# S5 scan in a hybrid decoder layer: a fifth step for each unit, and ScalarE copies into block form

## Chip, core and metric

The kernel runs on one core of one Trainium2 chip. The metric is the device time of one execution in microseconds; the profile beside it is one execution with its own time. In the views PE is TensorE, PEld its weight loads, DVE is VectorE, ACT is ScalarE, POOL is GpSimd, and SP is the engine that issues the loads.

## What is computed

One decoder layer on 512 tokens of width 2048 in float32. The change touches only the S5 mixer, a diagonal state space with 64 groups of 16 channels and 64 complex states per group. From the reference, cut:

```
A_bar = exp(A * dt);  B_bar = ((A_bar - 1) / A)[..., None] * Bm
Bu = einsum('gpc,btgc->btgp', B_bar, u)
states_t = A_bar * states_(t-1) + Bu_t
y = real(einsum('gcp,btgp->btgc', Cm, states)) + d * u
out = gelu(y) * sigmoid(gelu(y) @ w_glu + b_glu)
```

Beside it stand an mLSTM mixer (four heads), the common output projection, and a gated convolution MLP with two products of width 5504, which take most of the time.

## The kernel before

**The products.** Every large product is done in three passes of float32 (`mm3`, L207): a weight chunk of 128 x 1024 is loaded by SP (`wdma`, L142), ScalarE casts it to the high part, and VectorE subtracts to get the low part (`split`, L112, its rows are L115 and L116). `wget` (L160) splits two chunks ahead of the one that is multiplied, and three chunk buffers take turns. A chunk is 24 matmuls of 128 x 512. The stages are, in order: `u` (the S5 inputs), `xm`, `v`, `o`, `glu`, `ws` and `wm` (output projection, S5 part and mLSTM part), then the MLP (`gv`, `down`, `last`).

**The woven work.** After a chunk the loop calls `pump` (L193), which lets each generator in `side` do one step; a generator ends a step with `yield`. The S5 generator is `s5` (L454). It enters the list first and runs alone until stage `v`, from where two generators are served at each pump: `s5` and then `gates` (L671, the mLSTM gate products), later the `head` generators (L805). Nothing but these calls sets the order of the work: each engine gets its instructions in the order in which the code emits them.

**A unit of S5.** The loop at L575 goes over eight units (u = 0 to 7) of four groups of state pairs each, plus a last round u = 8 that only reads out. A unit has four steps; I name them A to D.

- A (L577 to L583): `taps` of the unit before (L566: PE turns Kt, L569 adds D on VectorE, five ScalarE copies L571 fill Tm), `u_turn` (PE turns the unit's inputs, ScalarE copies U), and `first` (L522): six small products on VectorE and then W by `cmul_to` (L513).
- B (L585 to L596): `readout` of the unit before (L544: twelve matmuls `py`, which need Sr, Si, the products with C of the unit before, and Tm), eight transposes `pw` of Wr and Wi with two ScalarE copies `xb`, and `second` (L536): the products of A and C (CAr, CAi), again by `cmul_to`.
- C (L598 to L621): sixteen matmuls `px`, six VectorE operations L611 to L616 on them with the phases Er and Ei that POOL makes ahead (`phases`, L463), and `turn_back` (L557, `pyt`).
- D (L623 to L640): matmuls `pkt`, two scans L629 and L630, and six products L633 to L638 that make Sr and Si.

`cmul_to` is called twice a unit. For each of its two outputs it multiplies twice into the buffers `t4[0]` and `t4[1]` (L516, L517) and then writes the sum or difference straight into block form, in which the two groups of a pair lie side by side on their own 64 partitions:

```
for k in range(2):
    p0 = slice(64 * k, 64 * k + 64)
    V.tensor_tensor(out=v5(o)[p0, :, :, k, :], in0=t4[0][p0], in1=t4[1][p0], op=op)
```

These are two instructions of 64 x 256 for each output (L520).

Of the kernel before, what the change touches and what calls it, by code (L numbers as in the profile page):

```python
# [53 lines left out]
def trunk(ctx: ExitStack, tc: tile.TileContext, A: dict, out: bass.AP):  # L54
    nc = tc.nc
    V, S, G, PE = nc.vector, nc.scalar, nc.gpsimd, nc.tensor
# [15 lines left out]
    def pair(i, dt):  # L72
        return sl.tile([P, 2 * T], dt, tag=f"p{i}", name=f"p{i}")
# [7 lines left out]
    p0, p1, p2 = [pair(i, F32) for i in range(3)]  # L81
# [4 lines left out]
    def slot(dt=F32, name="s"):  # L86
        q = mosubs if name in ("MOh", "MOl") else () if name == "acc" else subs[dt]
        if q:
            t = q.popleft()
            owner[id(t)] = (q, t)  # L90
        else:
            i = free.popleft()
            cnt[0] += 1
            t = sl.tile([P, T], dt, tag=f"s{i}", name=f"{name}_{cnt[0]}")
            owner[id(t)] = (i, t)
        return t

    def drop(*ts):
        for t in ts:
            i = owner.pop(id(t))[0]  # L100
            if isinstance(i, int):
                free.append(i)
            else:
                i.append(t)
# [25 lines left out]
    def vcol(n, i=0, w=1):  # L130
        c = VCOL[n] + i
        return vec[:, c:c + w]
# [307 lines left out]
    def v5(t):  # L440
        return t.rearrange("p (r j g c) -> p r j g c", r=4, j=4, g=2)

    def v3(t, n=4):
        return t.rearrange("p (r n) -> p r n", r=n)
# [9 lines left out]
    def s5():  # L454
# [38 lines left out]
        def fetch(u):  # L493
            bcs.append(slot(name="bc"))
            nc.sync.dma_start(out=bcs[-1][:, 0:256], in_=A["s5bc"][u])

        def coeffs(u):

            pr = slice(4 * u, 4 * u + 4)
            bc, ct = bcs.popleft(), slot(name="ct")  # L500
            if u < 7:
                fetch(u + 1)
            b4 = bc[:, 0:256].rearrange("p (q r c) -> p q r c", q=4, r=4)
            bt = bc[:, 256:512].rearrange("p (q r c) -> p q r c", q=4, r=4)
            t4 = [ct[:, i * 256:(i + 1) * 256].rearrange("p (r j c) -> p r j c", r=4, j=4) for i in range(2)]

            def pb(ap):
                return ap[:, pr].unsqueeze(2).to_broadcast([P, 4, 16])

            def ap4(ri):  # L510
                return afw[:, ri, pr, :].unsqueeze(3).to_broadcast([P, 4, 4, 16])

            def cmul_to(o_r, o_i, ar, ai, br, bi):  # L513
                br, bi = [x.unsqueeze(2).to_broadcast([P, 4, 4, 16]) for x in (br, bi)]
                for o, (x1, y1), (z1, w1), op in ((o_r, (ar, br), (ai, bi), SUB), (o_i, (ar, bi), (ai, br), ADD)):
                    V.tensor_tensor(out=t4[0], in0=x1, in1=y1, op=MUL)  # L516
                    V.tensor_tensor(out=t4[1], in0=z1, in1=w1, op=MUL)  # L517
                    for k in range(2):
                        p0 = slice(64 * k, 64 * k + 64)
                        V.tensor_tensor(out=v5(o)[p0, :, :, k, :], in0=t4[0][p0], in1=t4[1][p0], op=op)  # L520

            def first():  # L522
                w0r, w0i = W0
                V.tensor_tensor(out=bt[:, 0], in0=pb(w0r), in1=b4[:, 0], op=MUL)
                V.tensor_tensor(out=bt[:, 1], in0=pb(w0r), in1=b4[:, 1], op=MUL)
                V.tensor_tensor(out=bt[:, 2], in0=pb(w0i), in1=b4[:, 1], op=MUL)
                V.tensor_tensor(out=bt[:, 3], in0=pb(w0i), in1=b4[:, 0], op=MUL)
                V.tensor_tensor(out=bt[:, 0], in0=bt[:, 0], in1=bt[:, 2], op=SUB)
                V.tensor_tensor(out=bt[:, 1], in0=bt[:, 1], in1=bt[:, 3], op=ADD)
                cmul_to(Wr, Wi, ap4(2), ap4(3), bt[:, 0], bt[:, 1])  # L530
                for k in range(2):
                    p0 = slice(64 * k, 64 * k + 64)
                    S.activation(out=cd[p0, 0, :, k, :], in_=b4[p0, 2], func=AF.Copy)
                    S.activation(out=cd[p0, 1, :, k, :], in_=b4[p0, 3], func=AF.Copy, scale=-1.0)

            def second():  # L536
                cmul_to(CAr, CAi, ap4(0), ap4(1), b4[:, 2], b4[:, 3])
                V.tensor_tensor(out=v3(Dt[96:128, :]), in0=eye96[96:128, :].unsqueeze(1).to_broadcast([32, 4, 32]),
                                in1=vcol("d96", 4 * u, 4)[96:128].unsqueeze(2).to_broadcast([32, 4, 32]), op=MUL)
                drop(bc, ct)  # L540

            return first, second
# [23 lines left out]
        def taps():  # L566
            pk = aux_ps("pk")
            PE.transpose(out=pk[:, 0:P], in_=Kt, identity=ident)
            V.tensor_tensor(out=tm[:, :, 3, :], in0=v3(pk[:, 0:P]), in1=v3(Dt), op=ADD)  # L569
            for jo, d0, s0, n in ((2, 0, 32, 32), (2, 32, 64, 32), (2, 64, 96, 32), (1, 0, 64, 64), (0, 0, 96, 32)):  # L570
                S.copy(out=tm[d0:d0 + n, :, jo, :], in_=tm[s0:s0 + n, :, 3, :])  # L571
# [3 lines left out]
        for u in range(9):  # L575

            if u > 0:  # L577
                taps()
            if u < 8:
                u_turn(u)  # L580
                first, second = coeffs(u)
                first()
            yield  # L583

            if u > 0:  # L585
                yt = readout(u - 1)
            if u < 8:
                XB = []
                for w in (Wr, Wi):
                    pw = aux_ps("pw")  # L590
                    for r in range(4):
                        PE.transpose(out=pw[:, r * P:(r + 1) * P], in_=w[:, r * P:(r + 1) * P], identity=ident)
                    XB.append(slot(name="xb"))
                    S.copy(out=XB[-1], in_=pw)
                second()
            yield  # L596

            if u < 8:  # L598
                px = []
                for xb in XB:  # L600
                    p_ = aux_ps("px")
                    for r in range(4):
                        w = slice(r * P, (r + 1) * P)
                        PE.matmul(p_[:, w], lhsT=xb[:, w], rhs=U[u][:, w], start=True, stop=True)
                    px.append(p_)
                drop(*XB)
                Er, Ei, Rd = nxt
                if u < 7:
                    nxt = phases(u + 1)
                ta, tb, vr, vi = slot(name="ta"), slot(name="tb"), slot(name="vr"), slot(name="vi")  # L610
                V.tensor_tensor(out=ta, in0=px[0], in1=Er, op=MUL)  # L611
                V.tensor_tensor(out=vi, in0=px[0], in1=Ei, op=MUL)
                V.tensor_tensor(out=tb, in0=px[1], in1=Ei, op=MUL)
                V.tensor_tensor(out=vr, in0=ta, in1=tb, op=ADD)
                V.tensor_tensor(out=tb, in0=px[1], in1=Er, op=MUL)
                V.tensor_tensor(out=vi, in0=vi, in1=tb, op=SUB)  # L616
            if u > 0:
                turn_back(u - 1, yt)
            if u == 8:
                break  # L620
            yield  # L621

            pkt = aux_ps("pkt")  # L623
            for q, w in ((0, Wr), (1, Wi)):
                for r in range(4):
                    PE.matmul(pkt[32 * r:32 * r + 32, 0:P], lhsT=cd[:, q, r].rearrange("p g c -> p (g c)"),
                              rhs=w[:, r * P:(r + 1) * P], start=(q == 0), stop=(q == 1))
            S.copy(out=Kt, in_=pkt[:, 0:P])
            V.tensor_tensor_scan(out=ta, data0=Rd, data1=vr, initial=0.0, op0=MUL, op1=ADD)  # L629
            V.tensor_tensor_scan(out=tb, data0=Rd, data1=vi, initial=0.0, op0=MUL, op1=ADD)  # L630
            e0 = slice(0, P - 1)
            e_r, e_i, s_r, s_i, ra, rb = [v3(x)[:, :, e0] for x in (Er, Ei, ta, tb, vr, vi)]
            V.tensor_tensor(out=ra, in0=e_r, in1=s_r, op=MUL)  # L633
            V.tensor_tensor(out=rb, in0=e_i, in1=s_i, op=MUL)
            V.tensor_tensor(out=v3(Sr)[:, :, 1:P], in0=ra, in1=rb, op=ADD)
            V.tensor_tensor(out=ra, in0=e_r, in1=s_i, op=MUL)
            V.tensor_tensor(out=rb, in0=e_i, in1=s_r, op=MUL)
            V.tensor_tensor(out=v3(Si)[:, :, 1:P], in0=ra, in1=rb, op=SUB)  # L638
            drop(ta, tb, vr, vi, Rd, Er, Ei)
            yield  # L640
# [387 lines left out]
    for c in range(8):  # L1028
        wh, wl = wget()
        for j in range(4):  # L1030
            for q in range(2):
                k = 2 * c + q
# [398 lines left out]
    for m in range(MD, 16):  # L1431
        pt = acc_ps("down")
        for c in range(KD // 8):
            d_dma(j + 2)
            while spill:
                o, a = spill.popleft()
# [197 lines left out]
```

## Time and profile before

| what | value |
|---|---|
| median of 3 runs | 2118.34 us (2117.73 to 2120.08) |
| the profiled execution, its own time | 2120.67 us |
| its span, first to last instruction | 2118.9 us |
| mean granted clock of TensorE | 0.987 |
| busy: PE / DVE / ACT / POOL | 2067.7 / 1507.2 / 799.2 / 290.0 us |

The span is cut by stage below with one row for a stretch: busy time of each engine in it, the granted clock, and the load on the DMA engines. What PE isn't busy in a stretch it waited. S5 runs from about 80 to 354 us.

### The profile page before, as it was taken

What the parts mean: (1) busy time and instruction counts of PE and PEld (TensorE: products, weight loads), DVE (VectorE), ACT (ScalarE), POOL (GpSimd) and SP (SyncE); (2) the same over time, 40 slices, a digit from 0 to 9 for tenths busy, and PEclk for the clock granted to TensorE, in tenths of its full rate; (3) what the DMA queues carried; (4) which work ended last, traced back from release to release, by engine and by line L of the source; (5) the groups of instructions that cost most, each with busy time, mean ns of one, the idle gap of its engine ahead of it and who ended that gap; (6) DMA issues with size and microseconds to landing.
All of it is one profiled execution on the core that took longest, in us unless ns stands there. A gap on an engine that the chain in (4) does not pass through costs nothing.

```text
span 2118.9 us, 31328 instructions
## 1 busy us (share of the span) xinstructions
PE 2067.7 (98%) x12956; PEld 1881.7 (89%) x12956; DVE 1507.2 (71%) x2017; ACT 799.2 (38%) x946; POOL 290.0 (14%) x511
## 2 busy tenths in 40 slices
PE   8999989999999999999999999999999999999997
PEld 7887778888888799999999999999998888888887
DVE  7699996458655788989889898898886544222235
ACT  5244433345424543333443334333343432111124
POOL 4877660001101200000000000000000000000003
PEclk9999999999999989999999999999999999999999
DMA  4222113222333323333433333333332555333352
GB/s 172 83 73 76 63 53 110 82 87 80 115 139 115 136 103 119 111 110 114 135 110 110 120 120 119 120 110 111 118 131 90 188 174 190 110 110 113 119 199 80
DMA packets 75369, 244.73 MB, mean 115 GB/s; under 512 B 8397, under 2 KB 14029, under 8 KB 64217
## 3 DMA queue, kind: packets, MB, share of 16 engines
q1 hardware_dynamic: 75224, 242.72, 33.5%
q8 instruction: 101, 1.65, 0.3%
q14 instruction: 44, 0.35, 0.0%
HBM read 220.12 MB, written 22.57 MB: 115 GB/s over the span
## 4 chain that ended last, share of the span: by engine, by line
PE 80%; DVE 13%; POOL 2%; issue 2%; ACT 2%; DMA 1%; SPq 0%; DVEq 0%; ACTq 0%; POOLq 0%
PE gv L210 14%; PE gv L208 14%; PE gv L209 13%; PE down L209 7%; PE down L210 7%; PE down L208 7%; DVE a L116 2%; PE o L208 1%; PE ws L208 1%; PE ws L210 1%; PE o L210 1%; PE o L209 1%; PE ws L209 1%; PE v L208 1%; PE v L210 1%
## 5 line engine op out<-in xcount | busy, mean ns | idle before, releaser
L210 PE MATMUL gv<-T,a 128*128 128x256 f32 x2408 | 687.2, 285 | 4.4 <-DVE a L1157 4.4
L208 PE MATMUL gv<-T,a 128*128 128x256 f32 x2408 | 683.7, 284 | 4.0 <-ACT a L1153 4.0
L209 PE MATMUL gv<-T,a 128*128 128x256 f32 x2408 | 683.0, 284 | 0.0
L210 PEld LDWEIGHTS gv<-T,a 128*128 128x128 f32 x2408 | 463.9, 193 | 9.6 <-DVE a L1157 4.9
L208 PEld LDWEIGHTS gv<-T,a 128*128 128x128 f32 x2408 | 464.1, 193 | 4.5 <-ACT a L1153 4.5
L1153 ACT CAST a<-a 128x3584 fp32r<-128x3584 f32 x86 | 274.8, 3196 | 502.9 <-DVE a L1149 373.1
L209 PEld LDWEIGHTS gv<-T,a 128*128 128x128 f32 x2408 | 464.1, 193 | 0.0
L116 DVE TENSOR_TENSOR a<-a,a 128x1024 fp32r<-128x1024 f32 (+2 forms) x205 | 238.6, 1166 | 302.1 <-ACT a L115 301.1
L1157 DVE TENSOR_TENSOR a<-a,a 128x3584 fp32r<-128x3584 f32 (+2 forms) x88 | 336.2, 3822 | 82.7 <-ACT a L1153 82.6
L115 ACT CAST a<-a 128x1024 fp32r<-128x1024 f32 (+2 forms) x205 | 198.7, 973 | 379.6 <-PE down L209 296.1
L1486 POOL TENSOR_TENSOR c<-c,c 128x256 f32<-128x256 f32 x24 | 17.8, 741 | 1339.3 <-ACT c L1484 1338.4
L208 PE MATMUL down<-c,a 128*128 128x512 f32 x448 | 175.4, 392 | 4.0 <-ACT c L115 4.0
L210 PE MATMUL down<-c,a 128*128 128x512 f32 x448 | 175.0, 391 | 0.0
L209 PE MATMUL down<-c,a 128*128 128x512 f32 x416 | 162.9, 392 | 0.1
L1147 DVE TENSOR_TENSOR a<-a 128x1024 f32<-128x1024 f32 x86 | 104.8, 1219 | 0.0
L208 PEld LDWEIGHTS down<-c,a 128*128 128x128 f32 x448 | 84.6, 189 | 22.1 <-ACT c L115 4.4
L210 PEld LDWEIGHTS down<-c,a 128*128 128x128 f32 x448 | 84.7, 189 | 17.6
L209 PEld LDWEIGHTS down<-c,a 128*128 128x128 f32 x416 | 78.6, 189 | 16.9 <-DVE c L116 0.7
L209 PE MATMUL down<-a,a 128*128 128x512 f32 x176 | 68.5, 389 | 0.0
L208 PE MATMUL down<-a,a 128*128 128x512 f32 x176 | 68.5, 389 | 0.0
L1218 DVE SCALAR_TENSOR_TENSOR p<-p,vec,p 128x511 f32<-128x511 f32 x86 | 62.5, 748 | 2.5 <-ACT p L1211 0.9
L1149 DVE TENSOR_TENSOR a<-a 128x512 f32<-128x512 f32 x86 | 60.5, 703 | 2.9
(589 smaller groups left out, 3608.1 us busy)
## 6 DMA issues: line engine op xcount, KB each, us to landing
a<-in_wgv SPq DMA_DIRECT2D x86, 1024.0 KB, 4.8
a<-in_wdB SPq DMA_DIRECT2D x55, 512.0 KB, 3.4
a<-in_wdA SPq DMA_DIRECT2D x40, 320.0 KB, 3.2
hidd<-p SPq DMA_DIRECT2D x40, 256.0 KB, 6.2
a<-in_wxm SPq DMA_DIRECT2D x16, 512.0 KB, 3.3
a<-in_wv SPq DMA_DIRECT2D x16, 512.0 KB, 3.2
a<-in_wo SPq DMA_DIRECT2D x16, 512.0 KB, 3.2
a<-in_wouts SPq DMA_DIRECT2D x16, 512.0 KB, 3.5
```

The costliest lines, as they stand in the source:

```text
L115: S.copy(out=h, in_=src)
L116: V.tensor_tensor(out=l, in0=src, in1=f(h), op=SUB)
L208: PE.matmul(pt, lhsT=wh, rhs=xh, start=first, stop=False)
L209: PE.matmul(pt, lhsT=wh, rhs=xl, start=False, stop=False)
L210: PE.matmul(pt, lhsT=wl, rhs=xh, start=False, stop=last)
L1147: V.tensor_tensor(out=v[:, 4:6], in0=v[:, 0:1].to_broadcast([P, 2, T]), in1=v[:, 1:3], op=ADD)
L1149: V.tensor_tensor(out=v[:, 0], in0=v[:, 6], in1=v[:, 3], op=ADD)
L1153: S.copy(out=part(RH[s % 2], lo, hi - lo), in_=part(RS[s % 2], lo, hi - lo))
L1157: V.tensor_tensor(out=part(RL[s % 2], lo, hi - lo), in0=part(RS[s % 2], lo, hi - lo), in1=f(part(RH[s % 2], lo, hi - lo)), op=SUB)
L1218: V.scalar_tensor_tensor(out=y1[:, s:], in0=gs[:, 0:T - s], scalar=vcol("f_cw", 3 * (k0 + j) + 2 - s), in1=y1[:, s:], op0=MUL, op1=ADD)
L1486: G.tensor_tensor(out=x2, in0=x2, in1=sq[:, 0:HT], op=ADD)
```

## The change

Two edits. In `cmul_to` the sum or difference is made by one VectorE instruction of 128 x 256 in place, in `t4[0]`, and two ScalarE copies write it into block form; the two buffers change roles for the next output. In the loop a unit of u = 1 to 7 gets a second `yield` after step A, so that a pump passes in which S5 does nothing; I call this empty step E. Units 0 and 8 keep their steps.

```
                 for o, (x1, y1), (z1, w1), op in ((o_r, (ar, br), (ai, bi), SUB), (o_i, (ar, bi), (ai, br), ADD)):
                     V.tensor_tensor(out=t4[0], in0=x1, in1=y1, op=MUL)
                     V.tensor_tensor(out=t4[1], in0=z1, in1=w1, op=MUL)
+                    V.tensor_tensor(out=t4[0], in0=t4[0], in1=t4[1], op=op)
                     for k in range(2):
                         p0 = slice(64 * k, 64 * k + 64)
-                        V.tensor_tensor(out=v5(o)[p0, :, :, k, :], in0=t4[0][p0], in1=t4[1][p0], op=op)
+                        S.copy(out=v5(o)[p0, :, :, k, :], in_=t4[0][p0])
+                    t4.reverse()
...
                 first, second = coeffs(u)
                 first()
             yield
+            if 0 < u < 8:
+                yield
```

In the changed file the lines behind these edits are two to four further down: the new VectorE sum is L518, the ScalarE copies are L521, Tm's sum L569 is L571, its copies are L573, `py` is L550 to L552, `pw` L596, the split stays L115 and L116, the `xm` evacuation L752 is L756, its taps L757 are L761.

How the order moves, first on VectorE, between W of a unit and its products with C, in stage `xm` (`a_73` and `p_75` are Wr and Wi or CAr and CAi, `ct` holds t4, `a_70<-a_68,a_69` is the split of a chunk). Before:

```order
L520 TENSOR_TENSOR a_73<-ct_1991 64x16x16 x2
L516 TENSOR_TENSOR ct_1991<-a_73,bc_1702 128x256
L517 TENSOR_TENSOR ct_1991<-a_73,bc_1702 128x256
L520 TENSOR_TENSOR p_75<-ct_1991 64x16x16 x2
L116 TENSOR_TENSOR a_70<-a_68,a_69 128x1024
L752 TENSOR_TENSOR xs_2039<-xm,r_bc 128x512
L516 TENSOR_TENSOR ct_1991<-a_73,bc_1702 128x256
L517 TENSOR_TENSOR ct_1991<-a_73,bc_1702 128x256
L520 TENSOR_TENSOR a_73<-ct_1991 64x16x16 x2
```

Now:

```order
L518 TENSOR_TENSOR ct_2103<-ct_2103 128x256
L516 TENSOR_TENSOR ct_2103<-a_73,bc_1775 128x256
L517 TENSOR_TENSOR ct_2103<-a_73,bc_1775 128x256
L518 TENSOR_TENSOR ct_2103<-ct_2103 128x256
L116 TENSOR_TENSOR a_70<-a_68,a_69 128x1024
L761 SCALAR_TENSOR_TENSOR y_137_2083<-p_76,vec,y_137_2083 128x511
L761 SCALAR_TENSOR_TENSOR y_137_2083<-p_76,vec,y_137_2083 128x510
L761 SCALAR_TENSOR_TENSOR y_137_2083<-p_76,vec,y_137_2083 128x509
L116 TENSOR_TENSOR a_70<-a_68,a_69 128x1024
L756 TENSOR_TENSOR p_76<-xm,r_bc 128x512
L516 TENSOR_TENSOR ct_2103<-a_73,bc_1775 128x256
L517 TENSOR_TENSOR ct_2103<-a_73,bc_1775 128x256
```

One chunk's split stood between W and the products with C, and now there are two, with a tile's convolution taps between them.

ScalarE around step A: U's copy (L451), the C operand in block form (L533, L534; now L535, L536), then the cast of a chunk. Before:

```order
L571 COPY p_76<-p_76 32x4x32
L451 COPY p_76<-pu 128x512
L533 ACTIVATE a_73<-bc_1120 64x4x16
L534 ACTIVATE a_73<-bc_1120 64x4x16
L533 ACTIVATE a_73<-bc_1120 64x4x16
L534 ACTIVATE a_73<-bc_1120 64x4x16
L115 CAST a_69<-a_68 128x1024
```

Now:

```order
L573 COPY p_76<-p_76 32x4x32
L451 COPY U_1448<-pu 128x512
L521 COPY a_73<-ct_1450 64x16x16 x2
L521 COPY p_75<-ct_1450 64x16x16 x2
L535 ACTIVATE a_73<-bc_1124 64x4x16
L536 ACTIVATE a_73<-bc_1124 64x4x16
L535 ACTIVATE a_73<-bc_1124 64x4x16
L536 ACTIVATE a_73<-bc_1124 64x4x16
L115 CAST a_69<-a_68 128x1024 x2
```

The four copies of W stand behind Tm's copies and U's, and two casts follow in place of one.

ScalarE around step B: the read-out's copy (L553; now L555) and the two `xb` copies (L594; now L598). Before:

```order
L753 ACTIVATE y_101_1460<-xs_1459,vec 128x512
L553 COPY yt_1476<-py 128x4x4x32
L594 COPY xb_1483<-pw 128x512
L594 COPY xb_1490<-pw 128x512
L115 CAST a_69<-a_68 128x1024
```

Now:

```order
L757 ACTIVATE y_102_1531<-p_76,vec 128x512
L768 ACT_TABLE_LOAD
L768 ACTIVATE C_1534<-a_73 128x512
L555 COPY a_73<-py 128x4x4x32
L598 COPY xb_1555<-pw 128x512
L598 COPY xb_1562<-pw 128x512
L521 COPY a_73<-ct_1450 64x16x16 x2
L521 COPY p_75<-ct_1450 64x16x16 x2
L115 CAST a_69<-a_68 128x1024
```

The copies of CAr and CAi stand behind the read-out's copy and both `xb` copies, and in this unit a table load and an activation of the `xm` tile come ahead of all of them.

On TensorE, 48 matmuls of a stage (two chunks) now lie between `pu` and `py` of a unit where 24 lay, for units 1 to 7. S5's last read-out moves from stage `v` to stage `o`. The first `head` product follows two chunks later, and the last head's `pb` has 120 `ws` matmuls behind it before the first `wm` matmul, where 168 were.

## Rows read from the trace of the kernel before

**Rows 1.** The page: busy time by engine, and the chain that ended last by engine.

```profile
PE 2067.7 (98%) x12956; PEld 1881.7 (89%) x12956; DVE 1507.2 (71%) x2017; ACT 799.2 (38%) x946; POOL 290.0 (14%) x511
...
PE 80%; DVE 13%; POOL 2%; issue 2%; ACT 2%; DMA 1%; SPq 0%; DVEq 0%; ACTq 0%; POOLq 0%
```

**Rows 2.** Stretches: length, busy PE, PEld, DVE, ACT, POOL (counts), clock, DMA share, GB/s.

```profile
111.70:339.40 227.70, 211.76 (x1186) 180.33 (x1184) 218.62 (x381) 92.36 (x174) 145.66 (x269) 0.98 0.20 68
...
181.00:213.00 32.00, 29.45 (x170) 24.43 (x169) 31.09 (x51) 14.49 (x26) 22.02 (x41) 1.00 0.20 71
...
330.00:720.00 390.00, 390.00 (x1843) 325.77 (x1842) 234.96 (x403) 168.00 (x268) 43.34 (x31) 1.00 0.31 108
```

**Rows 3.** Waits of PE, 111.7 to 339.4 us: total, times, longest.

```profile
PE py L550 <- ACT p L571: 7.6, 5, 4.7
PE pw L592 <- DVE p L520: 5.3, 6, 1.1
PE pw L592 <- DVE a L520: 3.0, 3, 1.0
```

**Rows 4.** The chain of waits in one unit, 181 to 213 us, by line.

```profile
by line: DVE a L116 16.0%; DVE y L757 12.2%; issue 10.6%; DVE ct L517 5.9%; DVE a L520 5.0%; DVE xs L752 3.8%; DVE tb L630 3.7%; DVE ta L629 3.5%; ACT xb L594 3.0%; ACT a L115 3.0%; DVE ct L516 2.4%; DVE vr L614 2.3%; DVE vi L634 2.3%; DVE 
```

**Rows 5.** PE in order of time, step B of one unit: start, us, instruction, idle before.

```profile
211.77 0.49 PE L550 MATMUL py<-p,U 128*128 128x128 f32 x2 [0.48 <-ACT p L571]
...
215.28 0.63 PE L592 MATMUL pw<-ident,a 128*128 128x128 f32 x4 [1.01 <-DVE a L520]
216.96 0.73 PE L592 MATMUL pw<-ident,p 128*128 128x128 f32 x4 [1.06 <-DVE p L520]
```

**Rows 6.** The two half-clock stretches, and the wait ahead of the second.

```profile
217.30:220.80 3.50, 3.50 (x11) 2.82 (x10) 3.00 (x7) 2.09 (x4) 0.00 (x0) 0.51 0.40 150
...
313.80:320.00 6.20, 6.13 (x29) 6.13 (x30) 5.59 (x22) 3.48 (x9) 0.00 (x0) 0.52 0.00 0
...
313.87 0.79 PE L550 MATMUL py<-p,U 128*128 128x128 f32 x2 [4.67 <-ACT p L571]
```

**Rows 7.** DVE, 111.7 to 339.4 us: stretches of L520, L516, L517 alone; split; POOL wait.

```profile
111.70:339.40 227.70, 26.69 (x56) 0.98 0.20 68
...
111.70:339.40 227.70, 12.73 (x28) 0.98 0.20 68
...
111.70:339.40 227.70, 13.79 (x28) 0.98 0.20 68
...
L116 DVE TENSOR_TENSOR a<-a,a 128x1024 fp32r<-128x1024 f32 x28 | 36.3, 1298 | 0.6
...
DVE ta L611 <- POOL Er L484: 9.8, 1, 9.8
```

**Rows 8.** ScalarE groups, one unit (181 to 213 us); the last from 85 to 420 us.

```profile
L764 ACT ACT_TABLE_LOAD x1 | 1.3, 1283 | 0.0
L764 ACT ACTIVATE C<-y 128x512 f32<-128x512 f32 x2 | 1.3, 626 | 0.0
L571 ACT COPY p<-p 32x128 f32<-32x128 f32 x4 | 1.2, 296 | 6.8 <-DVE p L569 6.8
L594 ACT COPY xb<-pw 128x512 f32<-128x512 f32 x2 | 1.1, 590 | 0.0
...
L861 ACT CAST vv<-V 128x256 fp32r<-128x256 f32 x4 | 1.6, 396 | 0.0
```

**Rows 9.** DVE on the gate products (tile lsig): length, busy DVE, clock, DMA.

```profile
304.80:311.00 6.20, 5.47 (x18) 1.00 0.00 0
316.30:319.50 3.20, 2.67 (x15) 0.50 0.00 0
```

**Rows 10.** PE on tiles pb and wm: duration min/median/max, first and last start.

```profile
L925 PE MATMUL pb<-p,ones x24: 272/275/275, 500.2 to 609.6; 128*128 128x128 f32 x24
...
L208 PE MATMUL wm<-a,a x80: 389/389/395, 647.8 to 732.8; 128*128 128x512 f32 x80
...
L210 PE MATMUL wm<-MOh,a x48: 388/389/389, 651.6 to 735.3; 128*128 128x512 f32 x48
```

More of the change, by code (lines that the diff above doesn't have):

```diff
@@ L517, in cmul_to @@
                     V.tensor_tensor(out=t4[1], in0=z1, in1=w1, op=MUL)
+                    V.tensor_tensor(out=t4[0], in0=t4[0], in1=t4[1], op=op)
                     for k in range(2):
                         p0 = slice(64 * k, 64 * k + 64)
-                        V.tensor_tensor(out=v5(o)[p0, :, :, k, :], in0=t4[0][p0], in1=t4[1][p0], op=op)
+                        S.copy(out=v5(o)[p0, :, :, k, :], in_=t4[0][p0])
+                    t4.reverse()
             def first():
@@ L583, in s5 @@
             yield
+            if 0 < u < 8:
+                yield
             if u > 0:
```

## Prediction

> **What bounds the kernel now.** The page comes first: PE is busy 98% of the span, and the chain that ended last lies on PE for 80%, but on DVE for 13% [rows 1]. A kernel with so busy a PE gains only where PE waits, so the cut by stretches is next. From 330 to 720 us PE never waits [rows 2]. The stretch from the first to the last `taps` transpose of S5, 111.7 to 339.4 us, is another case: PE is busy 211.76 of 227.7 us, so it waits 15.9 us, while DVE is busy 218.62 us, 96% [rows 2]. The list of waits accounts for the whole of it: 7.6 + 5.3 + 3.0 = 15.9 us, all at step B, where `py` waits for Tm and `pw` for W [rows 3]. In one unit that looks as in [rows 5]: 0.48, then 1.01, then 1.06 us. The chain of such a unit runs over DVE almost throughout, its largest share the split of weight chunks [rows 4]. Here VectorE is the bound, and PE waits because W and Tm come at the end of a long VectorE queue. Weight chunks are not waited for at all in this stretch [rows 3].
>
> Two of these waits cost more than themselves. Behind them PE runs at the half level, 1.2 GHz: 3.5 us at a granted clock of 0.51 after the waits of [rows 5], and 6.2 us at 0.52 after the 4.67 us wait [rows 6]. The lost part is 3.5 x 0.49 + 6.2 x 0.48 = 4.7 us. So what PE can win in this stretch is at most 15.9 + 4.7 = **20.6 us**.
>
> **The empty step.** Seven more chunks now fall into the S5 stretch. A chunk takes PE 5.5 us (16 chunks of `wm` from 647.8 to 735.3 us plus the last matmul, 87.9 / 16 [rows 10]). The chunks are not added, they only come earlier, so nothing is paid for them later: 7 x 5.5 = 38.5 us move. A stretch without waits would take PE 227.7 - 15.9 - 4.7 + 38.5 = 245.6 us, 35.1 us for each of the seven units.
>
> VectorE must do its share in that time. It gets seven more splits at 1.30 us, 9.1 us [rows 7], and two evacuations of `v` of 128 x 512, which I take at 1.5 us together, between 0 and twice a split of 1.30 us, an instruction of double the width. Splits are made two chunks ahead, so a split that follows the empty step isn't urgent. In the step itself the queue of VectorE holds W first and the split after it: W and Tm are as early as before, and PE comes 5.5 us later. Where it waited 0.48 + 1.01 + 1.06 = 2.6 us it should now come about 3 us after W is ready.
>
> **The copies.** Over the seven units the 56 instructions L520 take 26.69 us [rows 7]. In their place stand 28 of 128 x 256 of the kind of L516 and L517, (12.73 + 13.79) / 56 = 0.47 us each [rows 7], 13.3 us together. VectorE saves 13.4 us and works 218.6 - 13.4 + 9.1 + 1.5 = 215.8 us of 245.6.
>
> ScalarE gets 56 copies of 64 x 256. No row shows one. The bounds are 0.296 us (128 columns, L571) and 0.59 us (512 columns, L594); I take 0.40 us, as L861 has at 256 columns [rows 8]. That is 22 us, and with seven casts about 30 us on 92.4 [rows 2]: half the stretch, no bound.
>
> The price is the hand-over. The second product of the next output writes the buffer that ScalarE still reads. With ScalarE free, VectorE waits for two copies, 0.8 us, less the one product that runs meanwhile: some 0.4 us, at two `cmul_to` a unit 14 x 0.4 = 5.6 us. VectorE is then taken for 221 of 245.6 us, 31.6 us a unit against 35.1. W itself reaches PE no later than before: a sum of 0.47 and two copies of 0.40 replace two L520 of 0.48. Behind the 0.4 us wait it is 0.2 to 0.8 us later, out of the 3 us.
>
> What is queued behind those waits? On VectorE at step A the next split, at step B the sum with D, a split, the taps of `xm`, and the operations of step C. On ScalarE the copies of CAr stand behind the read-out copy and two `xb` copies, hence behind PE's `pw`; in every second unit of `xm` also behind a table load and an activation, 1.28 + 0.63 us [rows 8]. There VectorE may wait up to some 3.6 us and begin step C up to 2 us late. In those units the taps lie behind W rather than ahead of it, so W is early and PE doesn't see it. Bounds of all hand-overs for PE: 0 and, with 0.8 us of every hand-over in PE's way, 5 us.
>
> A rule of the Trainium skill speaks against this place: "ScalarE: Activation LUTs", section "What ACT_TABLE_LOAD costs", gives 2.66 us for a switch of tables with the drain, while the trace has 1.28 us for the load. By the page the copies of CAr would come 1.4 us later in two or three units, and if nothing took that up the gain would be 3 to 4 us smaller. The sum goes by the row.
>
> **What else moves.** The gate products run by stage `v`, not by unit. Their first long piece, 5.47 us, and second, 2.67 us [rows 9], now both fall between step C and the taps of one unit (u = 5), where before the second lay behind the taps. That is the place of the 4.67 us wait [rows 6]. PE comes 5.5 us later there, the queue is 2.7 us longer and the late start of step C is mostly made up by the empty step before. I leave **2.6 us** of waits for this place and the hand-overs together; ends 0 and 4.7 plus its slow 3.0.
>
> The first unit keeps its steps; VectorE waits 9.8 us for POOL's phases in it [rows 7], so its copies cost nothing. POOL's phases for a unit take 22.0 us [rows 2] and have 35 us. The load of `bc` moves with step A, and the two loads of each head two chunks back; both sit in SP's queue ahead of weight loads, which no PE wait in the stretch is due to. The heads: the last `pb` is at 609.6 us, the first `wm` at 647.8 us [rows 10], 38 us, of which two chunks, 11 us, go. The 27 us left cover some ten VectorE operations of at most 1.3 us (a split has twice their width [rows 7]); without that cover they would cost up to 13 us.
>
> **The sum.** 20.6 - 2.6 = **18.0 us** off. The profiled execution's own 2120.67 us is 2.3 us above the median of 2118.34, perhaps by a slow stretch that not each run has. 18.0 off the one gives 2102.7, off the other 2100.3; I forecast **2101 us** against the median.
>
> **The rivals.**
>
> - Half of it (chance 0.14). The gate products keep their wait and slow stretch, 4.7 + 3.0 us, and the hand-overs cost PE 0.5 us a unit, 3.5 us. For it: both pieces now lie ahead of the taps. Against: the 5.5 us. Gain 20.6 - 11.2 = 9.4, 2109 us.
> - Slower (0.04). The hand-over ties VectorE to ScalarE and PE, and VectorE becomes longer than before. The old pace is reached when a unit takes (227.7 + 38.5) / 7 = 38.0 us. VectorE's work without waits is 215.8 / 7 = 30.8 us. If it stood idle at step B for the whole ScalarE queue ahead of CAr, 1.28 + 0.63 + 0.59 + 1.18 + 0.8 = 4.5 us (the read-out copy taken like an `xb` copy [rows 8]), and at A for five copies of Tm, U's and its own, 1.5 + 0.59 + 0.8 = 2.9 us, a unit takes 30.8 + 7.4 = 38.2 us, just slower than now; were the copies at their upper bound of 0.59 us, four of them 0.8 us more, it takes 39.0 us, 7 x 1.0 = 7 us longer: 2125 us. It decides from 7.2 us of waits a unit. Against it: VectorE has products of its own to do while ScalarE works through that queue.
> - No change (0.04). PE's waits go and the same number of microseconds comes back in `o` and `glu`, where the heads' products now fall two chunks later, beside other evacuations. Against: 390 us without a wait [rows 2] with DVE at 60%. 2118 us.
>
> **How the numbers follow.** My forecast has 0.78. Its own ends are 20.6 us with all gone, 2097.7, less 1.5 us of scatter between runs, and the half case at 2109; the range is **2096 to 2110**. Faster by over 0.2% (4.2 us, about what a measurement of this kernel can tell from none) is 0.78 + 0.14 = 0.92, the same 0.04, slower 0.04.
>
> **What would show it.** In the profile after, PE's waits at `py` and `pw` in S5 should fall from 15.9 to under 4 us, with `pw` now waiting for ScalarE's copy if at all; the stretch from the first to the last `taps` should take 246 to 250 us with DVE near 90%; the copies should be near 0.40 us; VectorE should wait for ScalarE at the second product. A DVE share that stays at 96%, or waits of PE for weight chunks in `xm`, would make it wrong.

## The result, and the profile after

The changed kernel takes 2131.66 us (median of 4 runs, 2129.51 to 2133.14), beside 2119.21 us for the kernel before (4 runs, 2117.73 to 2120.51). The ratio is 1.006, with a 95% interval of 1.0045 to 1.0075: 12.4 us slower, where 2101 us were forecast, and outside the range. The profiled execution took 2129.51 us with a span of 2127.7 us. The medians here and below are of fast runs, without two slow ones, 4162.10 us of e9 and 10014.46 us of e12. Names and lines below are those of the changed file.

First the page: busy time by engine, and the chain that ended last. They answer to [rows 1].

```profile
PE 2067.8 (97%) x12956; PEld 1879.4 (88%) x12956; DVE 1479.5 (70%) x1985; ACT 826.8 (39%) x1012; POOL 266.8 (13%) x511
...
PE 43%; DVE 41%; ACT 9%; issue 3%; POOL 2%; DMA 1%; SPq 0%; ACTq 0%; DVEq 0%; POOLq 0%
```

PE's work is the same, and VectorE has 28 us less of it over the whole span. Still the chain runs over VectorE for 41% of its length in place of 13%. The stretch from the first to the last `taps` transpose, by engines, answers to [rows 2] (length; PE, PEld, DVE, ACT, POOL; clock, DMA share, GB/s):

```profile
108.20:387.20 279.00, 253.37 (x1361) 211.85 (x1360) 209.98 (x368) 125.41 (x241) 124.89 (x269) 0.97 0.20 66
```

It took 279.0 us where 245.6 were forecast, and PE waits 279.00 - 253.37 = 25.6 us in it. VectorE is no longer busy all the time: 75%, not 96%. The transposes themselves, in PE's order of time, show when the loss begins (start, us, instruction, idle before):

```profile
108.23 0.28 PE L570 MATMUL pk<-ident,a 128*128 128x128 f32 x1
...
143.47 0.27 PE L570 MATMUL pk<-ident,a 128*128 128x128 f32 x1
...
178.31 0.33 PE L570 MATMUL pk<-ident,a 128*128 128x128 f32 x1 [0.21 <-ACT a L632]
...
258.54 0.33 PE L570 MATMUL pk<-ident,a 128*128 128x128 f32 x1 [1.99 <-ACT a L632]
...
349.29 0.48 PE L570 MATMUL pk<-ident,a 128*128 128x128 f32 x1 [7.83 <-ACT a L632]
```

The first two units take 35.2 and 34.8 us, which is the forecast's 35.1. The empty step works there as it was meant to. Later units do not keep that pace. PE's waits in this stretch (total, times, longest) answer to [rows 3]:

```profile
PE pk L570 <- ACT a L632: 10.0, 3, 7.8
...
PE v L209 <- DVE a L116: 5.2, 3, 3.4
...
PE xm L210 <- DVE a L116: 2.9, 3, 1.8
...
PE xm L208 <- ACT a L115: 1.5, 2, 1.2
...
PE pw L596 <- ACT p L521: 1.4, 2, 1.1
```

The old waits at `py` are gone and those at `pw` have shrunk. New ones stand at places that never waited before: the transpose of Kt (`pk`, behind ScalarE's copy L632), and the chunks of `xm` and `v`, behind their splits and casts. VectorE's own waits say more:

```profile
DVE a L116 <- ACT a L115: 31.4, 16, 2.9
...
DVE vi L616 <- POOL Ei L487: 12.6, 1, 12.6
...
DVE ct L517 <- ACT a L521: 11.7, 13, 3.5
...
DVE ct L516 <- POOL Ei L487: 4.6, 1, 4.6
```

Three kinds of wait: for ScalarE's cast of a chunk; for ScalarE's copies (the hand-over that the prediction priced); and twice for the last operation of POOL's phases. The longest, 12.6 us, in order of time on three engines:

```profile
327.13 0.11 POOL L469 MEMSET Rd<- 128x4 f32 x1 [21.54 <-ACT Rd L468]
...
340.96 0.73 POOL L487 TENSOR_TENSOR Ei<-gt 128x256 f32<-128x256 f32 x1
341.73 0.69 DVE L616 TENSOR_TENSOR vi<-px,Ei 128x512 f32<-128x512 f32 x1 [12.64 <-POOL Ei L487]
...
347.51 0.63 ACT L729 ACTIVATE F<-F 4x512 f32<-4x512 f32 x1 [15.84 <-DVE F L728]
348.05 1.03 ACT L115 CAST a<-a 128x1024 fp32r<-128x1024 f32 x1
348.99 0.25 ACT L632 COPY a<-pkt 128x128 f32<-128x128 f32 x1
```

This is step C of unit 6. The phases that POOL makes from 327.13 us are those of unit 7, which are due a unit later. Yet unit 6's `vi` waits until they are done. The reason is the place in memory. `slot` hands out the free buffer that was released longest ago, and `phases` releases its scratch buffer `gt` (it holds the half products of L482 to L486) as soon as its instructions are issued. Following `slot` and `drop` through the code: when `vi` of unit 6 is allocated, 5 free buffers remain in the kernel before, and 0 in the changed one. The round has become so short that `vi` gets the place of the `gt` released a moment ago, and must wait for POOL to read it for the last time. The `ct` of unit 5 gets the `gt` of an earlier call in the same way, the 4.6 us wait. S5 now reaches this step of unit 6 six chunks later, within stage `v`; by then four outputs of `v` and three buffers of the gate products are out as well, and two others, net, have come back.

Behind `vi` the queue carries it on. VectorE gets late to the gate products; ScalarE's exponential for them (L729) waits 15.84 us; the cast and the copy of Kt stand behind it; and PE waits 7.83 us at `pk`. Behind such places PE runs at the half level again, 1.2 GHz:

```profile
279.50:283.00 3.50, 3.48 (x8) 2.81 (x9) 3.00 (x6) 1.68 (x4) 0.00 (x0) 0.50 0.49 159
...
349.20:352.50 3.30, 3.21 (x10) 2.79 (x11) 3.30 (x3) 0.98 (x2) 0.00 (x0) 0.50 0.02 5
```

From 100 to 420 us, PE's idle time and what it lost at the half level (busy time times one minus the clock, summed over rows of 20 us) are 25.6 + 6.7 = 32.3 us, against 15.9 + 4.2 = 20.1 us before. The difference is 12.2 us, beside 12.4 between the medians. The two profiled executions themselves are only 8.8 us apart; the changed one lost 3.3 us less ahead of 80 us and 1.2 us less behind 720 us, where neither edit acts.

### The profile page after: what moved, and what is told of

It is laid out like the page before. It is cut to its first block, busy times and chain, and to the rows that moved or that the text cites. A ratio compares the mean times of both kernels' runs of the same rounds, so it can differ in the third digit from the quotient of the medians.

```text
span 2127.7 us, 31357 instructions
## 1 busy us (share of the span) xinstructions
PE 2067.8 (97%) x12956; PEld 1879.4 (88%) x12956; DVE 1479.5 (70%) x1985; ACT 826.8 (39%) x1012; POOL 266.8 (13%) x511
## 4 chain that ended last, share of the span: by engine, by line
PE 43%; DVE 41%; ACT 9%; issue 3%; POOL 2%; DMA 1%; SPq 0%; ACTq 0%; DVEq 0%; POOLq 0%
DVE a L1161 15%; PE down L209 7%; PE down L210 7%; PE down L208 7%; ACT a L1157 6%; DVE a L1151 4%; DVE a L1152 3%; DVE a L116 2%; DVE a L1153 2%; PE o L208 1%; PE ws L208 1%; PE o L210 1%; PE ws L210 1%; PE o L209 1%; PE ws L209 1%
## 5 line engine op out<-in xcount | busy, mean ns | idle before, releaser
L116 DVE TENSOR_TENSOR a<-a,a 128x1024 fp32r<-128x1024 f32 (+2 forms) x207 | 239.6, 1162 | 313.5 <-ACT a L115 313.1
L115 ACT CAST a<-a 128x1024 fp32r<-128x1024 f32 (+2 forms) x208 | 199.6, 966 | 359.9 <-PE down L209 296.6
L209 PEld LDWEIGHTS down<-c,a 128*128 128x128 f32 x416 | 78.8, 189 | 16.9 <-DVE c L116 0.7
```

The source lines that it names most:

```text
L115: S.copy(out=h, in_=src)
L116: V.tensor_tensor(out=l, in0=src, in1=f(h), op=SUB)
L209: PE.matmul(pt, lhsT=wh, rhs=xl, start=False, stop=False)
```

## Experiments

The trace suggests two theories. Theory 1: the longer S5 shortens the round of buffers. Theory 2: the copies couple VectorE and ScalarE, through the hand-over and through what stands behind the copies in ScalarE's in-order queue. All are medians; "against before" is the difference to the kernel before as it ran beside them (2118.22 for e1 to e4, 2118.84 for e5 to e8, 2118.32 for e9 to e12), and runs are compared by this difference.

| run | us | against before | ratio, 95% interval |
|---|---|---|---|
| e1 empty step alone | 2119.83 | +1.6 | 1.0001 to 1.0018 |
| e2 copies alone | 2136.25 | +18.0 | 1.007 to 1.0096 |
| e3 change, gt in a fixed place | 2119.62 | +1.4 | 0.9991 to 1.0009 |
| e4 before, gt in a fixed place | 2118.27 | 0.0 | 0.9992 to 1.001 |
| e5 empty step, gt fixed | 2111.00 | -7.8 | 0.9947 to 0.9975 |
| e6 copies one pump later, no empty step | 2135.76 | +16.9 | 1.0067 to 1.0093 |
| e7 change, gt fixed, copies one pump later | 2107.26 | -11.6 | 0.9937 to 0.9962 |
| e8 e5, and one more yield in the gates | 2116.70 | -2.1 | 0.9981 to 0.9999 |
| e9 change, gates later | 2123.07 | +4.8 | 1.0012 to 1.003 |
| e10 e7, gates later | 2099.72 | -18.6 | 0.9896 to 0.9922 |
| e11 e3, buffers of their own | 2113.99 | -4.3 | 0.997 to 0.9987 |
| e12 e7, gates held for empty steps | 2104.49 | -13.8 | 0.9919 to 0.9945 |

### One part alone: e1 and e2

e1 is the kernel before with the second `yield` only; e2 is the changed kernel without it:

```
             yield
-            if 0 < u < 8:
-                yield
```

> The kernel before with the empty step alone; VectorE still writes W and CA into block form. Its buffers take turns exactly as in the changed kernel: ct of unit 5 and vi of unit 6 come out of the round where POOL's scratch gt has just gone in. Theory 1 (short round of buffers): slow like the changed kernel, 2120 to 2135 us, with VectorE waiting for POOL L487 at vi of unit 6 (over 8 us) and at ct of unit 5. Theory 2 (the copies in ScalarE's queue hold up casts and hand-overs): without the copies the empty step brings its gain, 2100 to 2112 us.

> The changed kernel without the empty step: ScalarE's copies alone. Its buffers take turns as in the kernel before, gt comes back only an xb, xs or tile later in the next unit. Theory 1: no loss from buffers, VectorE has 13 us less to do, PE's waits at step B shrink: 2108 to 2119 us. Theory 2: the hand-overs and the casts behind the copies cost as in the changed kernel, 2122 to 2135 us.

e1 is 1.6 us slower than before, just below what theory 1 gave (2120 to 2135) and outside theory 2 (2100 to 2112); it is not as slow as the changed kernel. VectorE and PE, 100 to 420 us:

```profile
DVE vi L614 <- POOL Ei L487: 12.5, 2, 11.1
...
PE v L209 <- DVE a L116: 8.0, 3, 3.9
...
PE pkt L628 <- DVE vi L614: 5.8, 1, 5.8
...
DVE ct L516 <- POOL Ei L487: 4.7, 1, 4.7
```

The waits for POOL are there without any copy on ScalarE. So they belong to the empty step. The waits of [rows 3] shrank to 1.3 us (`pw`), which the buffers and the splits took back.

e2 went against theory 1's number (2108 to 2119) and just past the upper end of theory 2's: 18 us slower. So the copies have a harm of their own, larger than that of the whole change. Its waits in the same stretch:

```profile
DVE a L116 <- ACT a L115: 45.2, 20, 4.2
...
PE py L552 <- DVE bc L530: 7.6, 3, 2.6
...
PE pk L570 <- ACT a L630: 6.6, 4, 2.1
...
PE py L552 <- ACT p L573: 5.1, 3, 3.6
PE pw L594 <- ACT p L521: 4.6, 5, 1.4
```

VectorE waits 45 us for casts, 22 before. Those 22 us all lie behind the last `taps` (339 us); from the first to the last `taps` e2 has 25.6 us of such waits, and the kernel before at most 0.6. PE waits at steps A and B of S5, 25.7 us in all. (`py` does not read the DVE operation that its first row names. One of these waits ended at 186.12 us, and Tm's copies L573 at 184.54 + 1.52 = 186.06 us: as in the other `py` row, that one is the wait for Tm.) One `pk` wait shows the way, on ScalarE in e2:

```profile
210.72 0.82 ACT L755 ACTIVATE y<-xs,vec 128x512 f32<-128x512 f32 x1 [5.97 <-DVE xs L754]
211.56 1.28 ACT L766 ACT_TABLE_LOAD   x1
212.85 0.63 ACT L766 ACTIVATE C<-y 128x512 f32<-128x512 f32 x1
213.39 0.25 ACT L630 COPY a<-pkt 128x128 f32<-128x128 f32 x1
```

ScalarE stands idle for 5.97 us until VectorE has evacuated an `xm` tile, and Kt's small copy stands behind that, the table load and the activation. VectorE waits for ScalarE's casts, and ScalarE for VectorE. The Trainium skill, "Perfetto Trace Analysis", section "Optimizing Scalar/DVE Operations", says that moving work to ScalarE may make sense when VectorE is saturated. VectorE was at 96% [rows 2], and here it was not enough of a reason: e2 has less VectorE work and is slower.

### The place of gt: e3, e4, e5, e9

e3, e4 and e5 give `gt` the last 512 columns of the area of the chunk buffers, which are unused in this part of the program, so that it never goes into the round:

```
+        gt = part(aR1, 6)
         def phases(u):
...
-            er_, ei_, gt, Rd = [slot(name=n) for n in ("Er", "Ei", "gt", "Rd")]
+            er_, ei_, Rd = [slot(name=n) for n in ("Er", "Ei", "Rd")]
...
-            drop(gt)
```

> The changed kernel with one edit: POOL's scratch gt has a fixed place of its own (the unused end of the chunk buffers), and so never goes into the round. Theory 1: the waits of VectorE for POOL L487 at vi of unit 6 (12.6 us) and ct of unit 5 (4.6 us) are gone, with PE's 7.83 us wait at pk and the half clock behind both places, 11 to 19 us: 2112 to 2121 us. Theory 2: the buffers don't matter, 2128 to 2133 us.

> The kernel before with POOL's scratch gt in a fixed place of its own. Both theories: no wait of the kernel before is due to gt, so 2117 to 2121 us; a gain of more than 4 us would say that the fixed place helps in some other way, and the reading of the run with it in the changed kernel would have to take that off.

> The empty step alone (VectorE writes block form as before), with POOL's scratch gt in its fixed place. Against the run of the empty step alone, in which VectorE waited 11.1 us for POOL at vi of unit 6 and 4.7 us at ct of unit 5, and PE 5.84 us at pkt and 3.95 us at a split. Theory 1 (short round of buffers): these go with part of the half clock behind them, 6 to 12 us: 2108 to 2114 us, the gain that the empty step was meant to bring, less the gate products. Rival (the wait moves to the splits of VectorE, which is full anyway): 2117 to 2121 us.

e3 is 11.0 us below the changed kernel, each taken against its own runs of before; e4, the control, is the same as before. So the buffers account for about all that the change lost against the kernel before. They do not account for the rest: with `gt` out of the round the change is still no faster than before. PE's longest waits in e3:

```profile
PE v L209 <- DVE a L116: 8.8, 3, 4.1
...
PE xm L210 <- DVE a L116: 2.9, 3, 1.8
...
PE pk L571 <- ACT a L633: 2.1, 2, 2.0
```

The 12.6 and 4.6 us waits for POOL are gone, with the 7.83 us at `pk`. What is left, 18.3 us of PE idle, is near the 15.9 of before in size, but at other places. e5 says whose part that is: without the copies the empty step with `gt` fixed is 7.8 us faster than before, 9 us faster than e3. Against e1 the fixed place is worth 9.4 us, much as the 11.0 in the changed kernel. The only waits of PE in e5:

```profile
PE v L209 <- DVE a L116: 8.7, 3, 3.4
...
PE px L607 <- ACT xb L597: 1.5, 1, 1.5
```

e9 takes another road to theory 1, with nothing done to `gt`: the gate products enter the woven work later, so that fewer buffers are out (1 free at `vi` of unit 6, and not the one of `gt`).

```
-    side.append(gates())
     v_half(0)
+    side.append(gates())
```

> The changed kernel with one edit: the gate products enter the woven work after the first half of stage v, not ahead of it. Fewer buffers are then out while S5 runs, and vi of unit 6 no longer gets the place of gt (ct of unit 5 still does). Theory 1 (buffers): the 12.6 us wait at vi and PE's 7.83 us at pk go without any place of gt's own, 2131.7 less 6 to 13: 2118 to 2126 us. If the wait has another cause: 2129 us or more.

Its number is the one of theory 1: 7.7 us of the 12.4 are gone. The 12.6 us wait is gone with them, the 4.6 us wait at `ct` stayed. But the gate products moved too, and the same edit is worth 7.0 us in e10 (below), where `gt` is out of the round anyway. So e9 alone does not tell the two apart, and the case for the buffers rests on e3, e4 and e5. How e3's gain splits between the two places is not settled.

### The copies: e11, e7, e6

e11 adds to e3 a third buffer of 256 columns, so that the two outputs of a product have one each; the copies stay where they are. e7 adds to e11 that the copies are issued at the start of the next pump, behind the next chunk's cast:

```
-                    t4.reverse()
+                    t4[0], t4[2] = t4[2], t4[0]
...
-                    for k in range(2):
-                        p0 = slice(64 * k, 64 * k + 64)
-                        S.copy(out=v5(o)[p0, :, :, k, :], in_=t4[0][p0])
+                    outs.append((o, t4[0]))
...
+                def copies():
+                    for o, t in outs:
+                        for k in range(2):
+                            p0 = slice(64 * k, 64 * k + 64)
+                            S.copy(out=v5(o)[p0, :, :, k, :], in_=t[p0])
...
+                later.append(copies)
```

> The changed kernel with gt in its fixed place (2119.6 us) and a buffer of its own for the second output of a product, the copies where they were in ScalarE's queue. Rival A (the harm of the copies is the hand-over, VectorE's 14 us of waits at L518 for ScalarE): 2109 to 2115 us. Rival B (the harm is the order in ScalarE's queue, casts and copies of Kt behind copies that wait for VectorE): 2117 to 2121 us, with VectorE's wait at the split for the cast still near 40 us.

> The changed kernel with gt in its fixed place and with the copies issued one pump later, behind the next cast, from buffers of their own. Theory 2 (order in ScalarE's queue): VectorE's wait at the split for the cast falls from 41 us to under 15, PE's waits for splits of xm and v from 12 us to under 6, and the time from 2119.6 to 2104 to 2113 us. Rival (waits in the v stage come from the gate products and the evacuations on VectorE, not from the copies' place): 2115 to 2121 us.

> No empty step; ScalarE's copies alone, but each set is issued at the start of the next pump, behind the next chunk's cast, and the two outputs of a product have buffers of their own, so VectorE's sums wait for no copy; gt in its fixed place. The copies alone, in their old place, were 18 us slower than before. Theory 2 (the harm is the order in ScalarE's queue: casts, Kt's and Tm's copies behind copies that wait for VectorE, and VectorE behind the casts): VectorE's wait at the split for the cast falls from 48 us to under 20, and the time to 2112 to 2124 us. Rival (the harm is that W comes later and ScalarE has more to do, wherever the copies stand): 2130 us or more.

e11 is 5.7 us below e3, e7 another 7.3 us, each against its own runs of before. Both rivals of e11 hold a part: VectorE's waits of 13.7 us for the copies are gone and with them 5.7 us, and its waits for casts stayed (43.5 us). The order in ScalarE's queue is worth more. In e7 all that PE waits for is:

```profile
PE v L209 <- DVE a L116: 7.8, 3, 3.6
...
PE pw L607 <- ACT a L530: 0.7, 1, 0.7
...
PE pw L607 <- ACT p L530: 0.4, 2, 0.2
```

In stage `xm` nothing is left of the waits at `xm`, `pk`, `pkt` and `px` that e3 has. One expectation fell: VectorE's wait for casts did not go below 15 us; it is 37.5 us, near the 38.3 of e3. So that sum is no measure of the harm. It counts only where PE reaches a chunk sooner than its split. With the empty step, the copies in this form cost nothing and may earn something: e7's median is 3.7 us below e5's, but the two intervals overlap.

e6, the same without an empty step, is 16.9 us slower, where theory 2 had up to 5, and lies where its rival stood (2130 us or more).

```profile
PE pw L605 <- ACT a L530: 11.5, 5, 2.9
...
PE py L563 <- ACT p L584: 10.2, 5, 2.1
```

VectorE's wait for casts did fall, to 28.4 us (6.6 between 110 and 350 us), though not below the 20 that were expected. But issued one pump later, the copies of W come directly ahead of `pw`, which then waits up to 2.9 us for them, and VectorE still waits 7.9 us for copies at its next products. So e6 traded one delay for another and is no clean test of the order. With four steps to a unit, PE waited for W in both places that were tried for the copies (e2 and e6). How e2's 18 us divide between hand-over, order and the longer way of W stays open.

### The gate products: e8, e10, e12

e8 puts one more `yield` ahead of the gates' exponential in e5. e10 is e7 with e9's edit. e12 is e7 with the first piece and the exponential of the gate products held back until S5 is in an empty step, by a flag:

```
+        while not empty[0]:
+            yield
         z = tsc(fc, -1.0, MUL, o=new())
```

> The empty step alone with gt in its fixed place, and one more yield in the gate products, ahead of the exponential, so that its 18 small operations of VectorE fall into another pump than those ahead of it and what follows comes one pump later. If the wait of PE for the split behind the gate products (3.4 us and the half clock after it) hangs on which step of S5 they meet, the time moves by 2 to 6 us against the run without this yield, either way; if the VectorE work in stage v is too much wherever it stands, the same within 2 us.

> Empty step, copies one pump later from buffers of their own, gt in its fixed place (2107.3 us), and the gate products after the first half of stage v. If PE's three waits for splits of v (2.45, 3.57 and 1.81 us with some half clock) come from the gate products behind S5's work on VectorE, they go: 2099 to 2105 us. Rival: the heads, which wait for the gates, come too late for the products that need them, or the pile stands elsewhere: 2107 us or more.

> Empty step, copies one pump later from buffers of their own, gt in its fixed place (2107.3 us), and the gate products hold back their first piece and their exponential until an empty step of S5. If PE's three waits for splits of v come from gate products behind a full step of S5 on VectorE, most of 7.8 us and the 1.5 us of half clock go: 2099 to 2105 us. Rival (step D alone fills VectorE for too long): 2106 to 2109 us.

e7's longest wait, 3.57 us at a chunk of `v`, is that of a split behind step D's products and the gates' logarithm on VectorE; it starts late, behind this series:

```profile
293.70 3.34 DVE L334 SCALAR_TENSOR_TENSOR lsig<-lsig 128x16 f32<-128x16 f32 x9
297.18 1.23 DVE L116 TENSOR_TENSOR a<-a,a 128x1024 fp32r<-128x1024 f32 x1
```

e8 is 5.7 us slower than e5, within what was expected of it, but its trace gives another cause than the steps of S5. VectorE waits for POOL's `memset` of a small tile of the gate products, which now stands in POOL's queue behind the phases of a unit; PE's longest wait, 4.86 us at 332.65 us, is for the split of a chunk that comes behind it:

```profile
329.54 1.21 DVE L723 TENSOR_TENSOR_SCAN F<-one,gr 4x512 f32<-4x512 f32 x1 [10.89 <-POOL one L722]
```

In e10 and e12 PE waits for no chunk between 100 and 420 us; its idle time there is 1.3 and 1.4 us. From the first to the last `taps` transpose of e10, and the stretch behind it:

```profile
110.90:355.80 244.90, 243.62 (x1354) 207.17 (x1352) 211.40 (x357) 122.57 (x238) 138.03 (x266) 1.00 0.24 79
...
420.00:720.00 300.00, 295.48 (x1389) 246.43 (x1388) 206.35 (x366) 138.87 (x227) 49.06 (x34) 1.00 0.33 112
```

That is 244.9 us without a half-clock stretch: what the prediction had called a stretch without waits, 245.6 us. e10 beats both kernels by 18.6 us and 31.0 us. It gives 4.5 us back behind 420 us, since the heads come late: its last `pb` is at 626.0 us and its first `wm` at the same 626.0, with nothing between them. e12, at 2104.5 us, is in the range that was expected of it (2099 to 2105), at its upper end, and its S5 stretch is as clean. Its profile has 3.9 us of PE idle and 1.5 us lost at the half level from 420 to 720 us, little more than e10's 4.5 and 0.3; the 4.8 us between the two were not followed up.

## Why the prediction was wrong

**The bound, and what the empty step brings: right.** A stretch without waits was put at 245.6 us and a unit at 35.1; e10 measured 244.9, and the changed kernel's first two units 35.2 and 34.8. The gain that was forecast, 18.0 us, is what e10 has against before, 18.6. That the two agree so closely is in part luck: in the profiles e10 saves PE 18.9 us of idle and half-clock time from 100 to 420 us, loses 4.8 of them from 420 to 720, and has 4.7 us less of it in the rest of the span, which no edit touches. The change as it was made does not reach it, and four things stand between. From the changed kernel to e10 they are 11.0 (place of gt), 5.7 (hand-over), 7.3 (order of the copies) and 7.0 us (gate products), 31.0 together, where the sum had 2.6 us for all waits. Each figure is that of an edit made on top of those before it.

**Buffers: the largest step that failed.** "POOL's phases for a unit take 22.0 us and have 35 us" priced POOL at nothing. In units 1 to 7 of the changed kernel VectorE does not wait for Er and Ei, the results, but for the scratch buffer, which has no such slack once it goes back into the round. The prediction counted instructions and queues past which a step was moved, and never the buffers that are alive meanwhile. A longer S5 means more of them, and that could be counted without a chip: 5 free before, 0 after. With `gt` out of the round the change measures the same as before (e3), so this step makes the difference between slower and no change; the gain itself went to the next three.

**The hand-over: seen, mis-sized.** I put it at 14 x 0.4 = 5.6 us on VectorE and 0 to 5 us for PE, and took it into the 2.6 us. VectorE waited 11.7 us in 13 of the waits, the longest 3.5 us (3.6 was named as the most), and taking it away is worth 5.7 us of time (e11 against e3). "W itself reaches PE no later than before" does not follow from its own terms either: 0.47 + 2 x 0.40 = 1.27 us stand in place of 2 x 0.48 = 0.96. The copies themselves were sized right, 0.405 us where 0.40 was taken:

```profile
L521 ACT COPY a<-ct 64x256 f32<-64x256 f32 x28 | 11.3, 405 | 12.9 <-DVE ct L518 12.6
```

**What is queued behind the copies: the step left out.** I asked what stands ahead of the copies on ScalarE, and costed "seven casts" as busy time. Behind them stand the next casts, and Kt's copy comes in the same queue. ScalarE is busy for less than half of this stretch (125.41 of 279.00 us), and that share does not show it: while it waits for VectorE at a copy, the cast behind it waits too, and VectorE's split for the cast. It is worth 7.3 us (e7 against e11). The "slower" rival had this tie, at 7.2 us a unit of VectorE waits. It did not make the change slower by itself, since e3, with the tie and without the buffers, is at no change.

**The gate products: mis-sized.** "I leave 2.6 us of waits for this place and the hand-overs together; ends 0 and 4.7 plus its slow 3.0." They cost 7.0 us (e10 against e7, net of what e10 loses behind 420 us), near the upper end. `py` no longer waits there, as was read, but the splits of chunks stand behind the same pieces, and these have no empty step.

**Smaller points.** Waits for weight chunks in `xm` were named as what would make the forecast wrong, and they came. VectorE's 215.8 us of work in the stretch came out as 209.98. The 27 us left between the heads and `wm` are 656.7 - 629.4 = 27.3 us in the changed kernel. For the table switch the row's 1.28 us holds: in e2 the load starts at 211.56 and the next activation at 212.85 us, 0.01 us after the load's end. The Trainium skill ("ScalarE: Activation LUTs", "What ACT_TABLE_LOAD costs") adds some 1.38 us of drain to each switch; no such gap stands behind this load, nor ahead of it (the activation before it ends at 211.54 us). And to put the chance of slower at 0.04 was too sure for a change that moves seven chunks past a pool of buffers that I had not counted.

## What to carry to other kernels

When a change stretches one thread of woven work, count the buffers that are alive at its latest step, and look at which tile takes the place of a scratch buffer just released by a slower engine. When work is moved to an engine with an in-order queue, its busy share tells little (ScalarE was at 45% here): ask what stands behind the moved instructions, and whether it waits for the engine that was to be relieved. A change that loses may be the right one in the wrong surroundings: here each of four further edits, made one on top of the other, was worth 6 to 11 us, and with all four the gain that was forecast was there.

## What was not expected of the hardware

POOL's operations on 128 x 256 can take more than twice as long beside a busy VectorE. Here is the same line in the phases of units 6 and 7, and the engines around it (busy PE, PEld, DVE, ACT, POOL):

```profile
298.82 1.53 POOL L483 TENSOR_TENSOR gt<-Ei,a 128x256 f32<-128x256 f32 x1
...
338.19 0.61 POOL L483 TENSOR_TENSOR gt<-Ei,a 128x256 f32<-128x256 f32 x1
...
298.00:304.00 6.00, 6.00 (x31) 4.96 (x30) 5.97 (x6) 0.00 (x0) 5.84 (x5) 1.00 0.00 0
...
337.60:341.70 4.10, 3.86 (x17) 2.83 (x16) 0.00 (x0) 0.00 (x0) 3.84 (x6) 1.00 0.00 0
```

So POOL's 14 us in the long wait were its fast pace; VectorE stood still and POOL ran undisturbed. VectorE is slower too: the scan L633 took 1.63 us at 298.31 us and 1.22 at 350.25, where POOL was idle.

VectorE's busy share alone does not decide it. In the kernel before, VectorE was busy for 4.65 of 4.70 us from 210.30 us on, and POOL kept its pace:

```profile
210.93 0.61 POOL L483 TENSOR_TENSOR gt<-Ei,a 128x256 f32<-128x256 f32 x1
```

There VectorE's operations were short, and some of these grew: L526, on 128 x 64, took 0.63 us, and L525 just ahead of it, of the same shape, 0.21. The Trainium skill, "SBUF — State Buffer", section "Summary: rules for kernel authors", has it that of a VectorE operation with two SBUF inputs and a GpSimd operation that reads SBUF, the one that issues second is blocked until the first ends. These rows fit it: the engine with the short operations pays with the length of the other's. No run here separates this from other causes. Time saved on VectorE may then speed up POOL, which no term of the prediction had.
